# A hybrid attention trunk: a third early weight pair, gated linear attention as one stream, and later score scaling

## The chip, the cores and the metric

The kernel runs on one core of a Trainium2 chip. It is written as five instruction streams: PE (TensorE, matmuls and transposes into eight PSUM banks), DVE (VectorE), ACT (ScalarE), POOL (GpSimd) and SP (SyncE, which issues nearly all DMAs). The metric is the device time of one execution in microseconds; a profiled execution also gives a trace, whose span is a little shorter than the time.

## The reference

One layer over a sequence of 1024 tokens of width 1024, all in float32, cut to its core:

```python
h = rms_norm(x, pre_g)
qa, ka, va, ga, qb, kb, vb, gb, gk_low = split_columns(h @ w_in)     # 7184 columns

# 8 heads of differential softmax attention (two maps of width 64, values of 128)
w = softmax(causal(q1 @ k1.T)) - lam * softmax(causal(q2 @ k2.T))
oa = rms_norm(w @ va, subln_g) * (1 - lam_init) * silu(ga)

# 4 heads of gated linear attention (GLA; keys of 128, values of 256)
log_a = log_sigmoid(gk_low @ w_gk_up + b_gk) / 16
S_t = exp(log_a_t) * S_{t-1} + k_t^T v_t ;  o_t = q_t S_t
ob = rms_norm(o, gla_g) * silu(gb)

out = x + rms_norm(concat(oa, ob) @ w_out, post_g)
```

## The kernel before, in words

**Precision.** Every float32 operand of a large product is split into a rounded part `hi` (a cast by ACT) and the residue `lo` (a subtraction by DVE), and the product is three matmuls: hi by hi, lo by hi and hi by lo. A "residue" below is the DVE half of such a split, a "cast" the ACT half.

**Projections.** `h @ w_in` is computed by a scheme with seven products in place of eight for each 2x2 arrangement of blocks, numbered n = 1 to 7. The left operands are sums of blocks of h (`h11`, `h12`, `h22`, `s1` to `s4`), the right ones sums and differences of weight blocks. The *wide* steps (VB, VA: the values of GLA and of attention) multiply weight blocks of 512 columns, in two halves kk; their casts are L284, their residues L285, their differences L256. n = 6 needs a difference of its own tile, `w_t`. The *narrow* steps take a *pair*, two blocks of 128 columns of one kind: QA, KA, GA for attention's queries, keys and gates, QB, KB, GB for GLA's. A narrow step is 12 matmuls of 128x512 (L117). Its cast is L325, its residue L327; after it ACT copies the sum ("snap", L471) or DVE adds the parts, and `take` finishes them (L377 is the residue of the stored queries and keys, L381 their four DMA stores).

**Order of the work.** The list `order` fixes PE's order: four VB steps, then the early pairs' first two products, the rest of VB, VA, and then all other narrow steps. Pairs below `EARLY` = 2 load one 128-column half of their weights ahead of time (`load_early`, L220, tiles ks0 and ks1). `go(n)` does the next n steps and prepares the weights of about four steps to come; behind each narrow step it also advances one step of the stream in `fill`, and from pair `EARLY` on one step of loading, splitting and storing `w_out` (L644 to L652). The buffer of the raw weights, PSUM banks and the order in which each engine's code is written set the rest: each engine works through its own list and waits where a tile isn't ready.

**The gates of GLA.** `low_rank` (two matmul groups, the tiles gkl) and `decay(g)` (PE's `gk` from gkl, then ACT and DVE) run between the narrow steps, at 208 to 271 us.

**GLA.** `gla(g)` is a generator, one for each of four heads, chained into `fill`; each does two blocks (halves of the sequence): intra-chunk products `pa`, transposed keys `pk`, states `kv` (two groups), outputs `gpo` (two groups; ACT copies them to o at L904), and then the norm. The norm's mean over 256 channels is a matmul of `ones` with the squares: ACT squares both halves of o (L818, L821), DVE adds them, ACT casts the sum to `sq_hl` (L910), DVE takes the residue (L911), and after two more steps two matmuls of 128x512 give `gms`. Then ACT (L918, L920), DVE and ACT finish o, multiply by the gates and store hi and lo to `mixe` (L931, on SP). The tiles o and gates have one buffer each. The stream begins at the narrow step (7, 5); the first loads come at its first step.

**Scores and values.** After the last narrow steps the kernel merges by planned time three streams: the scores of all heads, the values, and the output product over the GLA half (`ypart`, from the tiles m_hi and m_lo that `mix` loads from `mixe`, L1000). For each block of 128 queries and each map m, PE makes the scores (`sc`), DVE adds the mask and finds the minimum in one instruction (L1109; the scores are negated), ACT takes the exponential with its sum (L1119). Then DVE takes the reciprocals of both sums (L1124), POOL scales the second map (L1125), and DVE scales the first and subtracts (L1128); the result is transposed on PE, cast and split (L1169) and multiplied by the values (`po`; the tiles v, loaded at L1060).

**The end.** From 942 us on the attention half of the output product (`yps`), the last norm and the stores.

Of the kernel before, what the change touches and what calls it, by code (L numbers as in the profile page):

```python
# [31 lines left out]
def hymba_kernel(  # L32
# [139 lines left out]
    pairs += [(n, h, c + h * P) for h in (2, 4) for n, c in (("KA", KA), ("QA", QA))]  # L172
# [18 lines left out]
    EARLY = 2  # L191
# [40 lines left out]
    def load_blocks(kind, *names):  # L232
        for name in names:
            r0, c0 = (512 * (int(i) - 1) for i in name)
            c0 += {"VA": VA, "VB": VB}[kind]
            for kk in range(2):
# [63 lines left out]
    def make_weights(i):  # L300
# [4 lines left out]
        if p in early and n < 3:  # L305
            src = early[p][n - 1]
        else:
# [384 lines left out]
    sums_of("s4")  # L692
    more_blocks("s1")
    go(1)
# [93 lines left out]
    low_rank()  # L788
    decay(0)
    go(4)  # L790
# [17 lines left out]
    go(order.index((4, 1)) - made[0])  # L808
# [6 lines left out]
    def mean_square(os, tile):  # L815

        sq = tile("sq")
        act.activation(sq, os[0], AF.Square)  # L818
        for o in os[1:]:
            sq2 = tile("sq")  # L820
            act.activation(sq2, o, AF.Square)  # L821
            dve.tensor_tensor(sq, sq, sq2, ALU.add)
        return sq

    loaded = {}

    def gla_loads(g, half):

        if g < GLA_HEADS and (g, half) not in loaded:
            cs = cols(half)  # L830
            kq = kp.tile([P, 2, 512], F32, tag="q0", name="kq")
            v = kp.tile([P, 4, 256], F32, tag="k0", name="gv")
            qd = kp.tile([P, 512], F32, tag="q1", name="gqd")
            sp.dma_start(kq[:, 0], gq_d[g][2, :, cs])
            sp.dma_start(kq[:, 1], gq_d[g][0, :, cs])
            c0 = g % 2 * 256
            sp.dma_start(v, gv_d[g // 2][:, half * 4 : half * 4 + 4, c0 : c0 + 256])
            sp.dma_start(qd, gq_d[g][1, :, cs])
            loaded[g, half] = kq, v, qd
        return loaded.get((g, half))  # L840

    def gla(g):

        u = None
        for half in range(2):
            cs = cols(half)
            kq, v, qd = gla_loads(g, half)
            gates = kp.tile([P, 2, 512], F32, tag="ks1", name="gg")
            o = kp.tile([P, 2, 512], F32, tag="ks0", name="go")
            an = kp.tile([P, 2, 4, P], F32, tag="k1", name="gan")  # L850
            a, kn = an[:, 0], an[:, 1]
            pa, ib = take_bank([P, 4, P], "pa")
# [8 lines left out]
            yield  # L861
            pk, ib = take_bank([P, 4, P], "pk")
            for i in range(4):
                tr(pk[:, i, :], kq[:, 0, i * P : i * P + P])
            free.append(ib)
            act.copy(kn, pk)
            for t in range(2):
                sp.dma_start(gates[:, t], gg_d[g][t, :, cs])
            yield
            us = [u]  # L870
            for m in range(2):
# [18 lines left out]
                yield  # L890
            for m in range(2):
# [15 lines left out]
            gla_loads(*((g, 1) if half == 0 else (g + 1, 0)))  # L907
            sq = mean_square([o[:, 0], o[:, 1]], t_c)
            hl = kp.tile([P, 2, 512], F32R, tag="k1", name="sq_hl")
            act.copy(hl[:, 0], sq)  # L910
            dve.tensor_tensor(hl[:, 1], sq, fp(hl[:, 0]), ALU.subtract)  # L911
            yield
            yield
# [656 lines left out]
```

## Time and profile before

| | |
|---|---|
| three runs, us | 1004.08, 1006.36, 1007.86 (median 1006.36) |
| profiled execution | 1009.11 us, its span 1007.4 us |
| mean granted PE clock | 0.989 |
| PE busy | 970.2 us, 4874 matmuls and transposes |
| DVE, ACT, POOL busy | 733.7, 586.3, 150.8 us |
| DMA | 219.86 MB, 218 GB/s |
| wide steps of the values | 14 to 190 us |
| GLA (pa to the last copy of o) | 333 to 581 us |
| scores | 637 to 941 us |
| end (yps) | 942 to 1000 us |

A row of a group of instructions gives line, engine, operation, the tile written and those read, the count, and then busy time with the mean of one and the idle time of the engine ahead of them with what ended it. "PE gms L117 <- ACT sq_hl L910: 3.9, 2, 2.6" says that PE idled 3.9 us in all ahead of gms, twice, at most 2.6 us, until ACT had written sq_hl. A row of the chain or of a timeline gives the start, the duration, and in brackets the wait ahead of it. DMA rows give the time of the issue and, where asked, the time from issue to landing. A clock of 0.50 means that PE was granted half of its full clock there.

### The profile page before, as it was taken

Reading aid. Unit: us, or ns where it says so; the run is one execution under the profiler, and the core shown is the slowest. Engines: PE = TensorE matmul, PEld = TensorE weight load, DVE = VectorE, ACT = ScalarE, POOL = GpSimd, SP = SyncE. Lnnn points to the kernel's source line nnn. Section 1 sums busy time; section 2 is a strip of 40 time slices with the busy share of each in tenths; the row PEclk is TensorE's granted clock in tenths of the full one; section 3 lists DMA queues with packets and bytes.
Section 4 is the critical chain, followed back from the end, with each engine's and each line's share of the span. In section 5 each row is a group of like instructions: output and inputs, shape, how many; then the busy total and the mean of one; then the engine's idle time right before and its main releaser. Section 6 shows DMA issues by size and latency. Waiting matters only on the chain.

```text
span 1007.4 us, 14826 instructions
## 1 busy us (share of the span) xinstructions
PE 970.2 (96%) x4874; PEld 812.4 (81%) x4874; DVE 733.7 (73%) x1442; ACT 586.3 (58%) x1144; POOL 150.8 (15%) x153
## 2 busy tenths in 40 slices
PE   6989999999999999999899999989999999999987
PEld 4868888778878788888788788778888888888765
DVE  6985476889898687777767884667777777887545
ACT  8631232455673587555566773457667667777663
POOL 5400000000000000001100100012222222343242
PEclk9999999999999999999999999999999999999999
DMA  9534333746657775898888789996575589974477
GB/s 335 181 93 150 122 110 104 234 135 193 235 180 257 234 240 193 273 297 268 252 262 251 230 253 324 310 350 187 164 230 199 178 286 369 275 200 91 128 219 136
DMA packets 155789, 219.86 MB, mean 218 GB/s; under 512 B 16208, under 2 KB 82768, under 8 KB 155616
## 3 DMA queue, kind: packets, MB, share of 16 engines
q1 hardware_dynamic: 151680, 211.57, 64.7%
q0 software_dynamic: 4032, 7.34, 4.8%
q8 instruction: 38, 0.62, 0.2%
q14 instruction: 39, 0.32, 0.1%
HBM read 133.41 MB, written 88.60 MB: 220 GB/s over the span
## 4 chain that ended last, share of the span: by engine, by line
PE 76%; DMA 9%; DVE 7%; ACT 3%; issue 2%; SPq 1%; POOL 1%; DVEq 0%; ACTq 0%; POOLq 0%
PE v L117 15%; PE x L117 13%; PE ypart L117 11%; PE y L117 8%; PE z L117 8%; PE sc L117 6%; PE po L117 4%; PE yps L117 4%; PE wtr L120 2%; PE gpo L117 2%; DMA v<-v_d 2%; PE kv L117 1%; DMA wo_raw<-in_w_out_dram 1%; DMA m_lo<-mixe 1%; PE gkl_ps L117 1%
## 5 line engine op out<-in xcount | busy, mean ns | idle before, releaser
L1119 ACT ACTIVATE p<-p,stt 128x896 f32<-128x896 f32 (+7 forms) x128 | 99.4, 777 | 47.2 <-DVE stt L1109 45.9
L327 DVE TENSOR_TENSOR w<-w_raw,w 128x512 fp32r<-128x512 f32 x136 | 94.4, 697 | 31.1 <-ACT w L325 30.9
L325 ACT CAST w<-w_raw 128x512 fp32r<-128x512 f32 x136 | 83.8, 620 | 51.1 <-PE y L117 31.9
L1109 DVE CUSTOM_DVE_ANT_0 p<-sc,maskt 128x512 f32<-128x512 f32 (+3 forms) x128 | 74.5, 585 | 31.4 <-PE sc L117 30.4
L1125 POOL TENSOR_SCALAR p<-p,stt,lam 128x1024 f32<-128x1024 f32 (+3 forms) x64 | 54.9, 863 | 241.5 <-DVE stt L1124 240.2
L117 PE MATMUL v<-w,s_hi 128*128 128x512 f32 x256 | 81.0, 396 | 3.7 <-ACT w L284 2.3
L117 PE MATMUL x<-s_hi,w 128*128 128x512 f32 x320 | 81.6, 398 | 0.7 <-ACT s L471 0.7
L117 PE MATMUL y<-h_hi,w 128*128 128x512 f32 x320 | 80.6, 394 | 0.0
L117 PE MATMUL z<-s_hi,w 128*128 128x512 f32 x320 | 80.5, 393 | 0.0
L117 PE MATMUL ypart<-wo_hi,m_hi 128*128 128x512 f32 x192 | 80.1, 417 | 0.0
L117 PE MATMUL ypart<-wo_hi,m_lo 128*128 128x512 f32 x192 | 76.4, 398 | 0.4 <-DMA m_lo<-mixe 0.4
L117 PE MATMUL ypart<-wo_lo,m_hi 128*128 128x512 f32 x192 | 76.2, 397 | 0.0
L117 PE MATMUL sc<-k,q 128*128 128x512 f32 (+1 forms) x192 | 71.2, 373 | 2.0 <-DVE stt L1109 2.0
L858 POOL TENSOR_SCALAR_AFFINE_SELECT gan<-gan 128x512 f32<-128x512 f32 x8 | 16.6, 2076 | 371.5 <-ACT gan L857 371.5
L117 PEld LDWEIGHTS x<-s_hi,w 128*128 128x128 f32 x320 | 59.8, 191 | 13.1 <-ACT s L471 1.1
L471 ACT COPY s<-x 128x512 f32<-128x512 f32 x60 | 35.0, 583 | 58.2 <-PE x L117 55.3
L117 PEld LDWEIGHTS z<-s_hi,w 128*128 128x128 f32 x320 | 59.1, 188 | 11.7
L117 PEld LDWEIGHTS y<-h_hi,w 128*128 128x128 f32 x320 | 59.0, 188 | 11.7
L117 PE MATMUL sc<-ks,q 128*128 128x512 f32 (+1 forms) x192 | 67.1, 351 | 0.0
L284 ACT CAST w<-w_block 128x1024 fp32r<-128x1024 f32 x24 | 25.1, 1052 | 69.1 <-PE v L117 39.8
L1128 DVE SCALAR_TENSOR_TENSOR p<-p,stt,p 128x1024 f32<-128x1024 f32 (+3 forms) x64 | 52.7, 826 | 15.8 <-POOL p L1125 15.3
L117 PEld LDWEIGHTS po<-wt_hi,v 128*128 128x128 f32 x320 | 54.1, 188 | 10.3 <-issue 2.2
(219 smaller groups left out, 2391.0 us busy)
## 6 DMA issues: line engine op xcount, KB each, us to landing
w_raw<-in_w_in_dram SPq DMA_DIRECT2D x40, 512.0 KB, 5.1
w_block<-in_w_in_dram SPq DMA_DIRECT2D x16, 512.0 KB, 4.4
k_d<-qk_st SPq DMA_DIRECT2D x64, 128.0 KB, 3.3
q_d<-qk_st SPq DMA_DIRECT2D x64, 128.0 KB, 3.4
wo_raw<-in_w_out_dram SPq DMA_DIRECT2D x32, 256.0 KB, 3.0
wo_d<-wo_hi SPq DMA_DIRECT2D x32, 256.0 KB, 2.8
wo_d<-wo_raw SPq DMA_DIRECT2D x32, 256.0 KB, 3.3
q<-q_d SPq DMA_DIRECT2D x32, 256.0 KB, 5.6
```

The lines of the kernel that those rows point to most:

```text
L117: tc.keep_in_program_order(pe.matmul(*a, **k))
L120: tc.keep_in_program_order(pe.transpose(dst, src, ident))
L284: act.copy(w[0], src)
L325: act.copy(w[0], src)
L327: split_last[:] = [dve.tensor_tensor(w[1], src, fp(w[0]), ALU.subtract)]
L471: act.copy(b[k], ps)
L858: pool.affine_select(a, a, [[0, 4], [1, P]], ALU.is_ge, 0.0, base=0, channel_multiplier=-1)
L1109: ins = dve.tensor_tensor_reduce(p[:, a:e], sc[:, : e - a], maskt[:, NZ + P - (e - a) :] if last else maskt[:, : e - a], 1.0, 3e38 if i == ...
L1119: act.activation(p[:, :n], p[:, :n], AF.Exp, bias=st[:, m : m + 1], scale=-1.0, accum_out=st[:, 2 + m : 3 + m],)
L1125: pool.tensor_scalar(p1[:, :n], p1[:, :n], st[:, 5:6], lam, ALU.mult, ALU.mult)
L1128: dve.scalar_tensor_tensor(p0[:, :n], p0[:, :n], st[:, 4:5], p1[:, :n], ALU.mult, ALU.subtract)
```

## The change

It has five parts.

1. *Early pairs.* `EARLY` is 3 and KA's second pair (heads 2 and 3) is the third early one, so its products 1 and 2 are the third couple of narrow steps between the wide steps of VB. Its early load uses the tile of pair 0 again and is issued once pair 0's second product is prepared. The wide blocks 12 and 22 are loaded kk by kk. `more_blocks` and the gates of GLA are shifted by some steps (`go`).
2. *GLA as one stream.* One generator `gla()` goes through the eight blocks. The first loads come two steps ahead of the first block, `pk` before `pa`, and the norm of a block (`gla_norm`) after the next block's `kv` groups, one step before its `gpo` groups. The tiles of o and gates are taken after that norm. The stream begins at step (8, 5).
3. *Squares.* The sum of the squares over 128 partitions is folded to 64; hi stands in the lower 64 partitions of one tile of 512 columns, lo in the upper 64, and one matmul replaces two. The tile is half of the next block's q tile.
4. *First values.* The values of the first head are loaded ahead of `mix(1)`.
5. *Scaling.* Reciprocal, POOL's scaling and DVE's scale and subtract of a block are issued when the next block's first minimum is (`scale_scores`).

The diff, cut to its core:

```diff
-    pairs = [("KA", 0, KA), ("QA", 0, QA), ("QB", 0, QB), ("KB", 0, KB), ("GB", 0, GB)]
+    pairs = [("KA", 0, KA), ("QA", 0, QA), ("KA", 2, KA + 256), ("QB", 0, QB), ("KB", 0, KB), ("GB", 0, GB)]
...
-    EARLY = 2
+    EARLY = 3
...
-        r = kp.tile([P, 2, HB, P], F32, tag=f"ks{p}", name="w_early")
+        r = kp.tile([P, 2, HB, P], F32, tag=f"ks{p % 2}", name="w_early")
...
     def load_blocks(kind, *names):
-        for name in names:
...
-            for kk in range(2):
+        for kk in range(2):
+            for name in names:
...
         if p in early and n < 3:
             src = early[p][n - 1]
+            if (p, n) == (0, 2):
+                load_early(2)
...
     sums_of("s4")
+    go(2)
     more_blocks("s1")
-    go(1)
+    go(2)
     more_blocks("s4")
...
     low_rank()
+    go(3)
     decay(0)
-    go(4)
+    go(5)
     decay(1)
...
+    def gla_norm(g, half, o, gates, hl):
+
+        ms, ib = take_bank([P, 512], "gms")
+        mm(ms, ones, hl, start=True, stop=True)
+        r = t_c("r")
+        act.activation(r, ms, AF.Ln, bias=eps_t, scale=1.0 / 256)
+        free.append(ib)
+        act.activation(r, r, AF.Exp, scale=-0.5)
...
+    def gla():
+
+        norm = None
+        gla_loads(0, 0)
+        yield
+        yield
+        for g, half in [(g, half) for g in range(GLA_HEADS) for half in range(2)]:
...
+            if norm:
+                gla_norm(*norm)
+                yield
+            gates = kp.tile([P, 2, 512], F32, tag="ks1", name="gg")
+            for t in range(2):
+                sp.dma_start(gates[:, t], gg_d[g][t, :, cs])
+            o = kp.tile([P, 2, 512], F32, tag="ks0", name="go")
...
-            hl = kp.tile([P, 2, 512], F32R, tag="k1", name="sq_hl")
-            act.copy(hl[:, 0], sq)
-            dve.tensor_tensor(hl[:, 1], sq, fp(hl[:, 0]), ALU.subtract)
+            hl = gla_loads(*((g, 1) if half == 0 else (g + 1, 0)))[2][:, 1]
+            sq, up2 = t_c("sq"), t_c("sq")
+            act.activation(sq, o[:, 0], AF.Square)
+            act.activation(up2, o[:, 1], AF.Square)
+            dve.tensor_tensor(sq, sq, up2, ALU.add)
+            act.copy(up2[:64], sq[64:])
+            dve.tensor_tensor(sq[:64], sq[:64], up2[:64], ALU.add)
+            act.copy(hl[:64], sq[:64])
+            dve.tensor_tensor(hl[64:], sq[:64], fp(hl[:64]), ALU.subtract)
+            norm = g, half, o, gates, hl
             yield
-            yield
-            ms, ib = take_bank([P, 512], "gms")
-            for i in range(2):
-                mm(ms, ones, hl[:, i], start=(i == 0), stop=(i == 1))
...
-    go(order.index((7, 5)) - made[0])
-    fill.append(chain(*(gla(g) for g in range(GLA_HEADS))))
+    go(order.index((8, 5)) - made[0])
+    fill.append(gla())
...
             if h == 0:
-                tc.keep_in_program_order(ins)
+                v_last[:] = [tc.keep_in_program_order(ins)]
...
-                if last and m:
-                    dve.reciprocal(st[:, 4:6], st[:, 2:4])
...
+                if last:
+                    c += scale_scores(ins)
+                    if m:
+                        unscaled.append((h, qb, n, st, p0, p1))
                 yield c
...
+    def scale_scores(after):
+
+        if not unscaled:
+            return 0.0
+        h, qb, n, st, p0, p1 = unscaled.pop()
+        with tc.issue_after(after.ins) if after else nullcontext():
+            dve.reciprocal(st[:, 4:6], st[:, 2:4])
+            pool.tensor_scalar(p1[:, :n], p1[:, :n], st[:, 5:6], lam, ALU.mult, ALU.mult)
+            dve.scalar_tensor_tensor(
+                p0[:, :n], p0[:, :n], st[:, 4:5], p1[:, :n], ALU.mult, ALU.subtract
+            )
+        w[h, qb] = p0
+        return 0.25 + n / 1024 * 1.4
...
             if e == E:
-                nxt = mix(1)
+                with tc.issue_after(v_last[0].ins):
+                    nxt = mix(1)
```

How it moves the instructions shows at three places. The first is ACT in GLA, around the norm of an early block (go is o, gg the gates, r the norm's factor). Before:

```order
L904 COPY go<-gpo 128x2x256
L818 ACTIVATE sq<-go 128x512
L821 ACTIVATE sq<-go 128x512
L471 COPY s<-x 128x512
L910 CAST sq_hl<-sq 128x512
L325 CAST w<-w_raw 128x512 x2
L471 COPY s<-x 128x512
L325 CAST w<-w_raw 128x512
L918 ACTIVATE r<-gms,eps_t 128x512
```

And now:

```order
L843 ACTIVATE r<-gms,eps_t 128x512
L845 ACTIVATE r<-r 128x512
L473 COPY s<-x 128x512
L327 CAST w<-w_raw 128x512
L852 CAST gg<-go 128x512 x2
L327 CAST w<-w_raw 128x512
L932 COPY go<-gpo 128x2x256 x2
L473 COPY s<-x 128x512
```

Before, the norm followed its own block's copies of o; now the norm of the block before stands directly ahead of the copies, which write the same tile o.

The second is SP at the start of the scores. Before:

```order
L381 DMA k_d<-qk_st 64x512 x4
L381 DMA q_d<-qk_st 64x512 x4
L1000 DMA m_hi<-mixe 128x1024
L1000 DMA m_lo<-mixe 128x1024
L1060 DMA v_5841<-v_d 128x1024
L1060 DMA v_5842<-v_d 128x1024
L950 DMA k_6030<-k_d 128x512 x2
```

And now:

```order
L383 DMA k_d<-qk_st 64x512 x4
L383 DMA q_d<-qk_st 64x512 x4
L1074 DMA v_5844<-v_d 128x1024
L1074 DMA v_5845<-v_d 128x1024
L1014 DMA m_hi<-mixe 128x1024
L1014 DMA m_lo<-mixe 128x1024
L964 DMA k_6024<-k_d 128x512 x2
```

The two loads of the first values and the two of `mix(1)` have changed places.

The third is DVE at the third block of the first head (ISA is the masked minimum, in two parts; wt_lo is the residue of transposed weights). Before:

```order
L1124 RECIPROCAL stt<-stt 128x2
L1169 TENSOR_TENSOR wt_lo<-wtr,wt_hi 128x512
L1109 ISA p_5964,stt<-sc,maskt 128x512
L1109 ISA stt 128x1
L1128 SCALAR_TENSOR_TENSOR p_5933<-p_5933,stt,p_5934 128x768
```

And now:

```order
L1124 ISA p_5963,stt<-sc,maskt,stt 128x128
L1124 ISA stt 128x1
L1152 RECIPROCAL stt<-stt 128x2
L1154 SCALAR_TENSOR_TENSOR p_5927<-p_5927,stt,p_5928 128x768
L1193 TENSOR_TENSOR wt_lo<-wtr,wt_hi 128x512
```

Before, this block's scaled product stood behind the next block's minimum and another product's residue; now it stands right behind its reciprocal, and both stand behind the minimum of the next block's first map.

More of the change, by code (lines that the diff above doesn't have):

```diff
@@ L805, in hymba_kernel @@
     dve.tensor_scalar(lam, lam, LAM_INIT, None, ALU.add)
-    go(order.index((4, 1)) - made[0])
+    go(order.index((5, 1)) - made[0])
     go(1)
@@ L812, in hymba_kernel @@
     decay(3)
[L815 to L823, printed above, removed]
     loaded = {}
     def gla_loads(g, half):
-        if g < GLA_HEADS and (g, half) not in loaded:
-            cs = cols(half)
[L831 to L849, printed above, removed]
+        if (g, half) not in loaded:
+            qh = kp.tile([P, 2, 512], F32R, tag="q1", name="gqd")
+            loaded[g, half] = [None, None, qh]
+            if g < GLA_HEADS:
+                cs = cols(half)
+                kq = kp.tile([P, 2, 512], F32, tag="q0", name="kq")
+                v = kp.tile([P, 4, 256], F32, tag="k0", name="gv")
+                sp.dma_start(kq[:, 0], gq_d[g][2, :, cs])
+                sp.dma_start(kq[:, 1], gq_d[g][0, :, cs])
+                c0 = g % 2 * 256
+                sp.dma_start(v, gv_d[g // 2][:, half * 4 : half * 4 + 4, c0 : c0 + 256])
+                sp.dma_start(fp(qh[:, 0]), gq_d[g][1, :, cs])
+                loaded[g, half][:2] = kq, v
@@ L860, in gla @@
             )
-            yield
[L862 to L868, printed above, removed]
             yield
```

69 lines of the change are left out of this document (35 added, 34 removed).

## The prediction

> **What bounds the kernel now.** I read the page first, then the waits of the matmul engine (PE), then the stages in which it idles. Three lines of the page:
>
> ```profile
> span 1007.4 us, 14826 instructions
> PE 970.2 (96%) x4874; PEld 812.4 (81%) x4874; DVE 733.7 (73%) x1442; ACT 586.3 (58%) x1144; POOL 150.8 (15%) x153
> PE 76%; DMA 9%; DVE 7%; ACT 3%; issue 2%; SPq 1%; POOL 1%; DVEq 0%; ACTq 0%; POOLq 0%
> ```
>
> PE is busy 96% of the span, so a change can win only where PE stands still, or by giving it fewer matmuls. The waits of PE over the whole run (us in total, times, longest):
>
> ```profile
> PE xT L120 <- DVE x L524: 9.2, 4, 7.7
> PE gms L117 <- ACT sq_hl L910: 3.9, 2, 2.6
> PE po L117 <- DMA v<-v_d: 2.8, 2, 2.0
> PE v L117 <- ACT w L284: 2.3, 1, 2.3
> PE sc L117 <- DVE stt L1109: 2.0, 3, 1.2
> ...
> PE v L117 <- DVE w L285: 1.3, 3, 0.8
> PE kv L117 <- DMA gv<-gv_d: 1.0, 1, 1.0
> ...
> PE gk L117 <- DVE gkl L753: 0.7, 1, 0.7
> ...
> PE gms L117 <- DVE sq_hl L911: 0.4, 2, 0.2
> ...
> PE pa L117 <- DMA kq<-gq_d: 0.3, 1, 0.3
> ```
>
> The first row is the start, which the change leaves alone. The other nine are each aimed at by one part of the change: together 3.9 + 2.8 + 2.3 + 2.0 + 1.3 + 1.0 + 0.7 + 0.4 + 0.3 = 14.7 us. That isn't all, as stretches of 3.41 us show (us, busy time of PE, PEld, DVE, ACT, POOL, granted PE clock, DMA share, GB/s):
>
> ```profile
> 57.33:60.74 3.41, 3.41 (x10) 2.63 (x9) 2.45 (x3) 0.93 (x1) 0.00 (x0) 0.50 0.58 133
> 490.82:494.23 3.41, 3.41 (x7) 2.44 (x8) 3.07 (x5) 2.78 (x5) 0.00 (x0) 0.50 0.86 259
> 555.67:559.08 3.41, 2.12 (x8) 1.53 (x9) 3.27 (x6) 3.39 (x7) 0.00 (x0) 1.00 0.59 189
> 647.84:651.25 3.41, 1.91 (x10) 1.21 (x9) 2.21 (x10) 1.19 (x3) 1.08 (x1) 1.00 0.79 184
> 651.25:654.66 3.41, 3.41 (x13) 2.83 (x12) 2.08 (x5) 2.21 (x5) 0.00 (x0) 0.50 0.89 251
> 661.49:664.90 3.41, 3.41 (x11) 2.62 (x10) 0.78 (x3) 0.91 (x2) 0.88 (x1) 0.50 1.03 311
> 668.00:940.00 272.00, 270.94 (x1581) 235.80 (x1580) 206.96 (x565) 192.20 (x425) 80.58 (x87) 1.00 0.72 221
> ```
>
> Four stretches run at clock 0.50, each right behind one of these waits; each gives PE half of 3.41 us of work and so costs another 1.7 us, 6.8 in all. A stretch in which PE was busy for 1.91 us was followed by one, a stretch with 2.12 us was not, so about 1.5 us of idle time in one stretch sets it off. The Trainium skill (TensorE: Matmul & The Clock Gate, HAM oscillation — how this bites in real kernels) states the rule as "no PE-idle gaps >~3.4µs". Here no gap of these stages is longer than 2.6 us and the clock fell nonetheless, so the trace speaks for the stricter reading; by the rule the clock would have nothing to give back. The last row tells that from 668 to 940 us PE idles for 1.1 us of 272: nothing is to be won there, only lost.
>
> **A third early pair.** Two more steps of 12 matmuls stand between the second early pair and the first difference weights w_t. PE and DVE there, from the chain and DVE's timeline:
>
> ```profile
> 41.63 2.74 PE x L117 x12
> ```
> ```profile
> 35.63 1.29 DVE L327 TENSOR_TENSOR w<-w_early,w 128x512 fp32r<-128x512 f32 x2
> 55.68 1.22 DVE L285 TENSOR_TENSOR w<-w_t,w 128x1024 fp32r<-128x1024 f32 x1 [0.51 <-ACT w L284]
> 57.96 0.68 DVE L377 SCALAR_TENSOR_TENSOR qk_st<-s,qk_st 128x512 fp32r<-128x512 f32 x1
> 68.78 1.22 DVE L285 TENSOR_TENSOR w<-w_block,w 128x1024 fp32r<-128x1024 f32 x1
> ```
>
> Two steps are 5.5 us of PE work that was done later in any case. DVE gets two residues of 0.65 us ahead of w_t, so w_t, finished at 56.9, comes at 58.2; PE, ready at 53.0, comes at 58.5. The waits there (2.3 and most of the 1.3) and the half clock behind them go, 5.3 us in reach. What is late next is the weights finished at 70.0 (the last row): DVE is 2.7 us later there (two residues, one sum, one 0.68 us residue of qk_st), PE only 58.5 + 10.9 - 69.0 = 0.4; one sum of 0.7 now follows instead of preceding them. I leave 1.0 us of wait: **-4.3**, between -5.3 and -2.6 (all of DVE's 2.7 us on the path). The early load shares the buffer of the first pair and is issued when DVE has read that, at about 37 us, ahead of the w_block loads of 45; its stores (four more SP issues) stand behind those loads. The wider order of those loads can only bring w_t earlier. A third x bank leaves one spare bank for the wide products instead of two; I price that at nothing, as the drains were done over 0.9 us before such a bank would be asked for, and a late drain costs its delay.
>
> **The low-rank gates.** Three steps (8.2 us) now stand ahead of the gk matmul: **-0.7**, at worst 0.
>
> **GLA.** The loads of the first block get two steps of cover, so the kq and gv waits go: **-1.3** (0 at worst). With hi and lo of the squares in two halves of one matmul, eight matmuls of 2.74 / 12 = 0.23 us fall away: **-1.8**. DVE and ACT get one small instruction more per block, off the path. The norm's matmul now stands behind the next block's four state products, about 20 us after its squares instead of two steps, so the gms waits (3.9 + 0.4) and the half clock of 490.82 go: -6.0. In return o and the gates, one buffer each, are handed from norm to next block within one step. The rows that price this: PE's wait and chain, then the tile `go` around that norm, then the landing of its stores (min, median, max) there and, last, over all blocks.
>
> ```profile
> 490.82 1.52 PE L117 MATMUL gms<-sq_hl,ones 128*128 128x512 f32 x2 [2.63 <-ACT sq_hl L910]
> ```
> ```profile
> 379.28 1.78 PE gpo L117 x16
> ```
> ```profile
> L931 SPq DMA_DIRECT2D mixe<-go x2: 394/461/528, 501.7 to 502.1; - x2
> ...
> DMA to landing us min/median/max: 2.7/2.8/2.9
> ```
> ```profile
> L904 ACT COPY go<-gpo x16: 566/577/588, 350.5 to 580.9; 128x512 f32<-128x512 f32 x16
> ...
> DMA to landing us min/median/max: 2.7/5.1/7.8
> ```
>
> The last store of that norm landed at 502.1 + 2.8, 14.1 us after its gms; with the slowest landing 19. In the new order ACT's copy of o waits for that, and behind it on ACT stand two squares, a snap, a cast and the copy of the next keys: about seven instructions of 0.6, 4 us. The keys are wanted six steps, two gpo groups, pk and pa after gms: 16.4 + 3.6 + 0.9 = 21 us. Usually 18 against 21 (no wait), at the slowest 23 against 21. Of seven hand-overs I charge +2.0 in all, between 0 and 7. GLA with the matmuls: **-7.1**, between -9.1 and -2.1.
>
> **First values ahead of mix.** SP issues (start, us) and the PE rows that want these loads; the landing row is m_lo's:
>
> ```profile
> 651.99 0.58 SPq L1000 DMA_DIRECT2D m_hi<-mixe  x1
> 652.61 0.44 SPq L1000 DMA_DIRECT2D m_lo<-mixe  x1
> 653.09 0.91 SPq L1060 DMA_DIRECT2D v<-v_d  x2
> ```
> ```profile
> DMA to landing us min/median/max: 5.0/5.0/5.0
> ```
> ```profile
> 659.33 0.35 PE L117 MATMUL po<-wt_hi,v 128*128 128x256 f32 x1 [1.99 <-DMA v<-v_d]
> 660.50 0.38 PE L117 MATMUL po<-wt_hi,v 128*128 128x256 f32 x1 [0.81 <-DMA v<-v_d]
> ...
> 665.52 0.40 PE L117 MATMUL ypart<-wo_hi,m_hi 128*128 128x512 f32 x1
> ```
>
> The values take the places of the mix loads and land by 657.6 instead of 660.5; PE wanted them at 657.3. So 2.8 us and the half clock of 661.49 go, 4.5 in reach. The mix loads then land at 660.5, and their first user, at 665.52, comes 4.5 us earlier, at 661.0: just in time. I charge +1.0: **-3.5**, between -4.5 and 0.
>
> **Scores scaled one block later.** DVE in this stage, by line, and one of its waits:
>
> ```profile
> L1128 DVE SCALAR_TENSOR_TENSOR p<-p,stt,p 128x1024 f32<-128x1024 f32 (+3 forms) x64 | 52.7, 826 | 15.8 <-POOL p L1125 15.3
> L1124 DVE RECIPROCAL stt<-stt 128x2 f32<-128x2 f32 x64 | 10.4, 162 | 19.5 <-ACT p L1119 19.1
> ```
> ```profile
> 645.52 1.28 DVE L1128 SCALAR_TENSOR_TENSOR p<-p,stt,p 128x1024 f32<-128x1024 f32 x1 [1.33 <-POOL p L1125]
> ```
>
> The reciprocal's wait for the exponential (19.5 us on DVE) mostly goes, but in the new order the reciprocal and the product that needs POOL's answer stand side by side in 39 of 64 blocks instead of 11, and each such pair waits about 1 us for POOL: some 30 us instead of 15.8. On DVE that cancels. On PE 2.0 us of sc waits and the half clock of 651.25 are in reach; but the first pair (645.52) waits as before, and the first transposes want a product that now stands behind one block more. **0**, between -3.7 and +2.0.
>
> **The sum.** -4.3 - 0.7 - 1.3 - 5.8 - 3.5 + 0 = -15.6, with -5.8 for gms (-6.0 - 1.8 + 2.0). The profiled execution took 1009.11 us (span 1007.4 and 1.7 around it) and would take 993.5. It is 2.75 us above the median of the three runs, 1006.36; the difference carried over to the median gives 990.8, forecast **991**.
>
> **Rivals.**
> 1. *Slower: ACT blocked at the copy of o.* For it: the order above, and stores that wait in SP's queue behind loads. Against: 18 against 21 us. It decides from a landing 17 us after gms on; at 20.5 PE would wait about 3.5 us in each of seven blocks and run a stretch at half clock after each: 7 x (3.5 + 1.7) = 36, less the 2.0 charged: 991 + 34 = 1025; slower than before from 2.5 us per block on. Chance 0.05.
> 2. *The stall moves from the values to the mix loads, and the scores cost 2.0.* For it: half a microsecond of room at 661.0, a DMA share of 1.03. Then 3.5 and 2.0 are lost: 996.5. Chance 0.17.
> 3. *The half clock isn't the waits' doing* (the reading of the rule above): it stays in the three stretches that I count as gone, 3 x 1.7: 996. Against it: all four stretches follow a wait. Chance 0.05.
> 4. *New waits eat it all*: the drains at one spare bank, and stores of the wo weights, which now start one pair later, among the loads before 635 us. The rows don't show such a wait; 1006. Chance 0.08.
>
> **How the numbers follow.** The forecast has 0.65. A measurement of this kernel can tell about 0.5% (5 us) from no change, so faster means under 1001.3. With rivals 2 and 3 that is 0.87, less a little for their upper ends: 0.86 faster, 0.09 same, 0.05 slower. With every term at its good end (-5.3 - 0.7 - 1.3 - 7.8 - 4.5 - 3.7 = -23.3) it is 983; the range runs from 984 to 1000, which takes in rivals 2 and 3 and leaves out 1 and 4.
>
> **What would show it.** Right: no gms wait, the v wait at w_t under 1.5 us, no po wait for v, clock 0.50 in at most two stretches between 50 and 700 us, 4866 matmuls. Wrong: waits at kv or pk for ACT, ypart waiting for m_hi or m_lo by over 2 us, or sc and wtr waits that sum to over 5 us from 640 to 940.

## The result, and the profile after

The changed kernel is slower: 1016.99 us in the median of 6 runs (1013.92 to 1020.77) against 1006.93 us of before (6 runs), a ratio of 1.0105 with a 95% interval of 1.0073 to 1.0137. The forecast was 991 us. The profiled execution took 1016.52 us, its span is 1014.8 us. Three lines of its page:

```profile
span 1014.8 us, 14875 instructions
PE 967.4 (95%) x4866; PEld 809.3 (80%) x4866; DVE 737.2 (73%) x1450; ACT 589.1 (58%) x1152; POOL 142.0 (14%) x153
...
PE 67%; DMA 17%; DVE 8%; ACT 4%; issue 3%; SPq 1%; POOL 0%; DVEq 0%; ACTq 0%; POOLq 0%
```

PE has its eight matmuls fewer and 2.8 us less work, but the span is 7.4 us longer: PE stands still 10 us more. In the chain of work that ended last (the third line) the share of DMA has gone from 9% to 17%. The waits of PE over the whole run (us in total, times, longest):

```profile
PE xT L120 <- DVE x L526: 8.5, 4, 7.1
PE ypart L117 <- issue: 5.5, 1, 5.5
PE gms L117 <- DVE gqd L943: 4.7, 2, 4.1
PE kv L117 <- ACT go L932: 3.3, 1, 3.3
PE kv L117 <- DMA gv<-gv_d: 2.7, 1, 2.7
PE yps L117 <- ACT yps L1447: 2.2, 2, 1.9
PE sc L117 <- DMA ks<-k_d: 2.1, 2, 1.5
PE wtr L120 <- DVE p L1154: 1.7, 1, 1.7
...
PE sc L117 <- DVE stt L1124: 1.4, 1, 1.4
...
PE v L117 <- DVE w L285: 0.5, 1, 0.5
```

Of the rows at which the change was aimed, v at the weights of ACT, gk, po for v and kq are gone, v at DVE is 0.5 instead of 1.3. In their place stand new rows, in two stretches of the program.

**GLA.** The new waits kv <- ACT go (3.3) and gms (4.7) belong to one ring: from the norm's matmul over its stores, the copy of o and its squares to the next norm's matmul. The third, kv <- gv (2.7), comes by another path (run 7). The waits of ACT between 340 and 640 us, after and then before, name the ring's closing point:

```profile
ACT go L932 <- DMA mixe<-go: 24.8, 6, 7.8
```
```profile
ACT go L904 <- DMA mixe<-go: 1.0, 1, 1.0
```

In six of the seven hand-overs ACT stood in front of the copy of o until the stores of the norm before had landed. The hand-over with the longest landing, first on ACT's timeline, then on PE's:

```profile
557.71 0.59 ACT L879 COPY gan<-pk 128x512 f32<-128x512 f32 x1
564.71 1.07 ACT L932 COPY go<-gpo 128x512 f32<-128x512 f32 x2 [6.41 <-DMA mixe<-go]
```
```profile
565.35 1.16 PE L117 MATMUL kv<-gv,gan 128*128 128x128 f32 x8 [3.30 <-ACT go L932]
573.04 0.47 PE L117 MATMUL gms<-gqd,ones 128*128 128x512 f32 x1 [0.59 <-DVE gqd L943]
597.59 0.63 PE L117 MATMUL gms<-gqd,ones 128*128 128x512 f32 x1 [4.13 <-DVE gqd L943]
```

The norm's matmul before this copy was at 540.8; the last store of o landed 23.8 us later. Over the seven blocks it was 13.5, 16.3, 17.1, 18.7, 18.9, 23.8 and 16.4 us. Then come the copies, two squares, the fold and the residue, and with them the next gms can run: from one gms to the end of the residue for the next the ring takes 22 to 32 us, and a block without waits has some 28.5. The first row of ACT shows that the block's keys had been copied ahead of the copy of o here, so it wasn't the keys that PE waited for at kv. That the copies had to free a PSUM bank for kv would explain the row, but isn't shown. The last row, 4.13 us, is the ring at the last block, which has only two plain steps ahead of its norm.

**Start of the scores.** The two parts of `mix(0)` are issued at 633.4 and 634.6 us and land 9.8 and 9.9 us later, behind ten loads of wo, each of 512 KB. PE waits 5.5 us for the first (the profile names "issue", but m_hi lands at 643.2 and the matmul starts at 643.27). Stretches of 3.41 us (us, busy time of PE, PEld, DVE, ACT, POOL, granted PE clock, DMA share, GB/s):

```profile
560.25:563.66 3.41, 1.79 (x8) 1.14 (x7) 0.00 (x0) 0.00 (x0) 0.00 (x0) 1.00 1.07 370
563.66:567.07 3.41, 1.72 (x12) 1.59 (x13) 0.70 (x2) 2.36 (x5) 0.00 (x0) 1.00 0.91 269
567.07:570.49 3.42, 3.42 (x19) 2.87 (x18) 3.42 (x5) 2.83 (x6) 0.89 (x1) 1.00 0.64 236
...
594.38:597.79 3.41, 0.20 (x1) 0.21 (x2) 3.35 (x7) 3.28 (x7) 0.00 (x0) 1.00 0.26 98
597.79:601.20 3.41, 3.41 (x9) 2.63 (x9) 3.41 (x6) 3.19 (x7) 0.00 (x0) 0.50 0.47 157
...
638.72:642.13 3.41, 0.00 (x0) 0.00 (x0) 0.69 (x1) 0.46 (x1) 0.00 (x0) 1.00 1.02 417
642.13:645.54 3.41, 1.81 (x4) 1.14 (x5) 0.00 (x0) 0.00 (x0) 0.00 (x0) 0.51 0.75 263
645.54:648.96 3.42, 3.42 (x10) 2.65 (x9) 0.70 (x2) 0.00 (x0) 0.00 (x0) 0.50 1.02 292
```

The half clock is gone from 57 and 490 us, where the waits went, and has come behind the new ones (597.79; two stretches from 642.13). While PE stood still from 638.72 to 642.13 the DMA engines were full.

### The profile page after: what moved, and what is told of

Read it like the earlier page. It is cut to its first block, busy times and chain, and to the rows that moved or that the text cites. A ratio compares the mean times of both kernels' runs of the same rounds, so it can differ in the third digit from the quotient of the medians.

```text
span 1014.8 us, 14875 instructions
## 1 busy us (share of the span) xinstructions
PE 967.4 (95%) x4866; PEld 809.3 (80%) x4866; DVE 737.2 (73%) x1450; ACT 589.1 (58%) x1152; POOL 142.0 (14%) x153
## 4 chain that ended last, share of the span: by engine, by line
PE 67%; DMA 17%; DVE 8%; ACT 4%; issue 3%; SPq 1%; POOL 0%; DVEq 0%; ACTq 0%; POOLq 0%
PE v L117 12%; PE ypart L117 11%; PE x L117 10%; PE z L117 7%; PE y L117 6%; PE sc L117 6%; PE po L117 5%; PE yps L117 4%; PE wtr L120 3%; DMA mixe<-go 2%; DMA v<-v_d 2%; DMA wo_d<-wo_raw 2%; DMA wo_raw<-in_w_out_dram 2%; DMA m_lo<-mixe 2%; DMA ks<-k_d 1%
## 5 line engine op out<-in xcount | busy, mean ns | idle before, releaser
L329 DVE TENSOR_TENSOR w<-w_raw,w 128x512 fp32r<-128x512 f32 x134 | 91.4, 686 | 27.2 <-ACT w L327 26.7
L327 ACT CAST w<-w_raw 128x512 fp32r<-128x512 f32 x134 | 82.6, 619 | 39.4 <-PE y L117 19.0
L256 DVE TENSOR_TENSOR w_raw<-w_raw 128x512 f32<-128x512 f32 x80 | 55.9, 699 | 11.2 <-DMA w_raw<-in_w_in_dram 10.2
L117 PE MATMUL v<-w,h_hi 128*128 128x512 f32 x192 | 60.3, 401 | 0.7 <-ACT h_hi L567 0.7
L887 POOL TENSOR_SCALAR_AFFINE_SELECT gan<-gan 128x512 f32<-128x512 f32 x8 | 7.1, 888 | 383.7 <-ACT gan L886 383.7
```

Source lines behind the costliest of these rows:

```text
L117: tc.keep_in_program_order(pe.matmul(*a, **k))
L256: dve.tensor_tensor(dst, a, b, ALU.subtract)
L327: act.copy(w[0], src)
L329: split_last[:] = [dve.tensor_tensor(w[1], src, fp(w[0]), ALU.subtract)]
L887: pool.affine_select(a, a, [[0, 4], [1, P]], ALU.is_ge, 0.0, base=0, channel_multiplier=-1)
```

## The experiments

All ratios are against the kernel before on the same chip, with 95% intervals; 0.1% is 1.0 us. "A" is the changed kernel. The parts taken one by one, each on the kernel before (the stream with its folded squares, which were not tried by themselves; the last row is two parts together):

| run | ratio | interval |
|---|---|---|
| early_pair_alone (with w_out earlier) | 1.0019 | 0.9989 to 1.0048 |
| stream_as_changed | 1.0033 | 1.0008 to 1.0059 |
| stream_norm_first | 0.9939 | 0.9907 to 0.9972 |
| values_alone | 0.9948 | 0.9919 to 0.9978 |
| scores_alone | 1.0048 | 1.0027 to 1.0068 |
| early_and_values | 1.0019 | 0.9997 to 1.0041 |

And from A on, one edit after the other:

| run | ratio | interval |
|---|---|---|
| A | 1.0105 | 1.0073 to 1.0137 |
| wout_from_early | 1.0095 | 1.0054 to 1.0136 |
| gla_as_before | 1.0080 | 1.0047 to 1.0112 |
| norm_before_states | 1.0016 | 0.9981 to 1.0050 |
| wout_and_norm | 0.9988 | 0.9953 to 1.0023 |
| mix_ahead_of_values | 0.9986 | 0.9966 to 1.0006 |
| mix0_ahead_of_wo | 0.9987 | 0.9964 to 1.0010 |
| scores_in_two_steps | 1.0070 | 1.0039 to 1.0101 |
| scores_as_before | 0.9926 | 0.9898 to 0.9953 |
| best_again (the same kernel) | 0.9953 | 0.9934 to 0.9973 |
| best_mix_first | 0.9963 | 0.9942 to 0.9983 |
| best_mix0 | 0.9956 | 0.9935 to 0.9978 |
| two_kept_alone | 0.9951 | 0.9931 to 0.9972 |

The theory ahead of the first runs: the hand-over of o (H) and the later stores of w_out (W) make the new waits. Rivals stand in each expectation.

**1. w_out earlier.** The prediction's fourth rival named the stores of w_out, which start one pair later.

```diff
-            if order[i][0] >= EARLY:
+            if order[i][0] >= EARLY or order[i][1] in (5, 6):
                 wo_step(order[i][1])
```

> The changed kernel, but the early pairs' products 5 and 6 also advance the steps that load, split and store w_out, so that the last store of w_out comes a few narrow steps earlier than in the kernel before instead of one pair later. Theory W (the late stores of w_out stand on SP ahead of the loads of wo, and these hold back m_hi): the matmul ypart waits under 1.5 us for m_hi instead of 5.5, the half clock there goes, 1017 - 8 = 1009 us. Rival N (SP is held by the ks loads, whose tiles are those of the last block's o and gates, so by the late last norm): ypart still waits 4 us or more, 1015 to 1017 us.

1017.45 us, no gain. PE waits at ypart for 2.5 + 0.8 us here, less than in A though more than W had it, but the time is that of A: W is refused as the cause. Rival N, with 4 us or more at ypart, isn't borne out either. What was gained at ypart doesn't reach the end, a first sign of what follows under 5.

**2. The norm ahead of the next states.** Two steps earlier, with the same number of steps in a block:

```diff
             yield
+            if norm:
+                gla_norm(*norm)
+                yield
             us = [u]
             for m in range(2):
...
-            if norm:
-                gla_norm(*norm)
-                yield
             gates = kp.tile([P, 2, 512], F32, tag="ks1", name="gg")
```

> The changed kernel, but the norm of a block stands ahead of the next block's two state groups (kv) instead of behind them, two steps earlier. Theory H (the hand-over of o: ACT's copy of o waits until the stores of the norm before have landed, 24.8 us in six copies, and that ripples on to kv, gms and the clock): ACT waits under 8 us at these copies, PE's waits for kv <- ACT go (3.3), gms (4.7) and the half clock behind (1.7) go, 1007 to 1009 us, and the last norm is about 8 us earlier. Rival S (the squares are then the late ones, with three steps less behind them): gms waits of 1 to 3 us in most blocks, 1015 to 1025 us.

1007.09 us: by the ratios 9 us less than A, for a norm two steps earlier. The waits of PE from 330 to 635 us in this kernel (the first is at the end of that time, at ypart):

```profile
PE ypart L117 <- DMA wo_d<-wo_hi: 4.8, 1, 4.8
...
PE gms L117 <- DVE gqd L943: 1.6, 3, 1.1
...
```

The kv waits are gone and gms is down to 1.6. But ACT still waits 21.7 us at the copies (seven, at most 4.8), not under 8 as expected: the copies follow the landing here too, only that PE doesn't meet them. The theory's place was right, its picture of how the wait goes was not: the copies still wait, but PE comes to what hangs on them later than they do.

**3. GLA of before, and both edits.** The first takes GLA's functions from the kernel before, the second has both edits above.

```diff
-    fill.append(gla())
+    fill.append(chain(*(gla(g) for g in range(GLA_HEADS))))
```

> The changed kernel with the GLA of the kernel before (one generator for each head, norm behind its own block, two matmuls for its squares); the other parts stay. Theory H: the stream costs 7 us more than the old one, and part of the wait for m_hi hangs on its late last norm: 1006 to 1010 us. If only the stores of w_out set that wait, 1010 us with ypart waiting 4 to 5 us; if the last norm sets it, 1002 us with ypart waiting under 1 us.

1013.37 us, above all its cases: A without its stream is still 8 us slower than before, and PE waits 3.6 us for m_hi. So the late last norm isn't the only cause of that wait.

> Both edits, w_out from the early pairs on and the norm ahead of the states. Theories W and H together: 1017 - 8 - 9 = 1000 us. If the transfers between 605 and 645 us are bound by the DMA engines themselves (share 1.0) and not by the order of the issues, ypart still waits 3 us or more and the time is 1004 us or more.

1004.14 us, and PE still waits 2.7 + 0.9 us at ypart. The second case holds: the transfers stay late.

**4. The scores.** The base is wout_and_norm (1004 us), with the scaling of before:

```diff
-                if last:
-                    c += scale_scores(ins)
-                    if m:
-                        unscaled.append((h, qb, n, st, p0, p1))
+                if last and m:
+                    dve.reciprocal(st[:, 4:6], st[:, 2:4])
...
```

> The kernel with w_out from the early pairs on and the norm ahead of the states (1004 us), and in it the scaling of the scores as in the kernel before. Theory P (the later scaling costs PE the waits sc <- DVE stt 1.4 and wtr <- DVE p 1.7 at the start of the scores, ks waits of 2.3 with a half clock near 860 us, and 1 us at the end): those rows go, 999 us. Rival: the waits only change their name (sc <- DVE stt three times, 2.0, as before), 1004 us.

999.21 us, the expected time, 0.6% under its base; but these are four runs, and twelve more of the same kernel (best_again, run 5) are 0.35% under it, with intervals that overlap. Of the rows that theory P names, ks fell from 2.3 to 0.8 us and yps <- yps from 2.1 to 0.8; wtr only changed its name (1.7, now 1.9 <- DVE stt). By itself on the kernel before:

> The kernel before with the later scaling of the scores alone. Theory P (DVE now waits for POOL in 40 of 64 blocks, 39 us in place of 14 plus 19 for the reciprocal, and PE meets the start and the end of the scores later for it): 1007 + 5 = 1012 us, with waits at sc, wtr and yps of over 5 us where there were 3.3. Rival (the later scaling costs only where PE is ahead of its transfers, which it isn't in the kernel before): 1006 to 1008 us.

1012.17 us: 0.48% slower, clear of noise (2.7 to 6.8 us). The waits of PE that have grown behind 700 us, with the later scaling (in an execution of 1008.19 us):

```profile
PE sc L117 <- DMA ks<-k_d: 1.7, 1, 1.7
PE yps L117 <- ACT yps L1431: 2.0, 1, 2.0
```

The first is at 864 us, the second at 941, with a clock of 0.83 from 940 to 950. In the kernel before PE waits nowhere from 850 to 900 us, and at most 0.7 us at yps <- yps. A and wout_and_norm, which have the later scaling too, show the same two places (1.5 and 1.9, 2.3 and 2.1). Counted by the matmuls in the trace, this kernel is 25 ahead of before at 850 us and 3 at 950; wout_and_norm is 3 ahead of scores_as_before at 850 us and 29 behind at 950. So it is there that the later scaling loses time. At the first transposes of scores_alone PE doesn't wait. How the later product delays the ks load isn't shown. The third run parts the reciprocal from the product by another minimum:

```diff
+                if last and not m:
+                    scale_second(ins)
-                if last:
+                if last and m:
                     c += scale_scores(ins)
-                    if m:
-                        unscaled.append((h, qb, n, st, p0, p1))
+                    unscaled.append((h, qb, n, st, p0, p1))
```

> The 1004 us kernel (w_out from the early pairs on, norm ahead of the states, later scaling), with the later scaling in two steps: reciprocal and POOL's product behind the next block's first minimum, DVE's product behind its second. Theory P1 (the later scaling costs because reciprocal and product stand side by side and DVE waits 39 us for POOL): DVE's waits for POOL fall under 10 us with the reciprocal's still under 5, and the time is at or under that of the kernel with the old scaling, 996 to 999 us. Rival P2 (it costs because the product, and with it the transposes, comes one block later): 1004 us or more, with DVE's waits gone all the same.

1016.19 us, worse by 0.8%. DVE's waits from 640 to 935 us, of its base wout_and_norm and of this kernel:

```profile
DVE p L1154 <- POOL p L1153: 39.4, 40, 1.4
DVE p L1124 <- PE sc L117: 23.0, 39, 2.4
```
```profile
DVE p L1124 <- PE sc L117: 56.1, 78, 3.1
...
DVE p L1162 <- POOL p L1154: 6.9, 17, 0.9
```

and PE's largest wait from 600 us on there:

```profile
PE po L117 <- DVE wt_lo L1202: 6.7, 8, 1.6
```

DVE's 39.4 us at POOL shrink to 6.9, as the theory P1 wanted, and the kernel is slower. P1 as it was put falls: taking these waits away gave no time back. The run doesn't price them by themselves, as the product is later still in this kernel, by one map's minimum. The cost has grown with that, which speaks for P2. How the later product gets to PE (a values stream that trails the scores, with fewer matmuls to cover it; the row of po) is argued from one profile, not shown.

**5. Where the early pair's time goes.** The early pair by itself, with its `go` counts, and w_out as in 1:

```diff
-    EARLY = 2
+    EARLY = 3
...
-            if order[i][0] >= EARLY:
+            if order[i][0] >= EARLY or order[i][1] in (5, 6):
```

> The third early pair alone, with w_out from the early pairs on; GLA, values and scores as before. PE has 5 us less of waits by 220 us. Theory G (the transfers from 600 to 645 us give the end of the narrow steps its time, so that what PE gains ahead of them is waited off at ypart): ypart waits 3 us or more for m_hi, 1004 to 1006 us. Rival: the gain comes through, 1001 us or less.

1010.9 us. The matmuls of ypart and po, before and then with the pair (the shortest, median and longest in ns, the first and last start in us), and PE's wait at po with the pair:

```profile
L117 PE MATMUL ypart<-wo_hi,m_hi x192: 387/397/628, 635.4 to 937.1; 128*128 128x512 f32 x192
...
L117 PE MATMUL po<-wt_hi,v x320: 220/280/384, 659.3 to 959.3; 128*128 128x256 f32 x128, 128*128 128x128 f32 x32
```
```profile
L117 PE MATMUL ypart<-wo_hi,m_hi x192: 387/397/629, 631.2 to 939.1; 128*128 128x512 f32 x192
...
L117 PE MATMUL po<-wt_hi,v x320: 220/280/582, 659.0 to 961.7; 128*128 128x256 f32 x128, 128*128 128x128 f32 x32
```
```profile
PE po L117 <- DMA v<-v_d: 5.1, 2, 4.5
```

PE comes to the scores 4.2 us earlier and starts the values 0.3 us earlier: it waits 5.1 us for v, where it waited 2.8. The expected place was ypart, it was po; that the lead is given back at transfers is as theory G has it. But the time is above G's 1004 to 1006 us: from the first po to the last this kernel loses another 2.7 us, and that isn't explained. The next two kernels differ in the pair and the w_out edit: the stream with its norm ahead of the states, the folded squares, the values first and the old scaling, without the two and with them.

> The kernel before with GLA as one stream (norm ahead of the states), the folded squares and the first values ahead of mix; no third early pair, scores as before. It is the 999 us kernel without the early pair and without the change to w_out. Theory G (the transfers from 600 to 700 us set when the scores run, and what the early pair gains ahead of them is waited off): ypart doesn't wait for m_hi, 999 to 1001 us. Rival (the early pair's 5 us come through): 1004 us.

> The kernel that took 999 us (early pair, w_out from the early pairs on, norm ahead of the states, folded squares, values first, scores as before), in more rounds. 0.74% under the kernel before, with an interval of 0.3% either way; without the early pair it was 0.49%. Theory G (the early pair's gain is waited off): 0.4 to 0.6%, 1003 us; rival (it comes through where the rest is mended): 0.7 to 1.0%, 999 us.

1002.52 us and 1002.54 us, 0.9951 and 0.9953: the pair is worth nothing here, within some 0.3%, as G has it (whose 999 to 1001 us for the kernel without it were too low). The 999 us of scores_as_before, the same kernel, came from four runs; the two intervals overlap. PE's waits from 600 to 720 us, with the pair and then without it:

```profile
PE ypart L117 <- DVE qk_st L379: 2.3, 1, 2.3
PE wtr L120 <- DVE stt L1139: 1.9, 1, 1.9
PE ypart L117 <- DMA m_lo<-mixe: 1.3, 1, 1.3
PE sc L117 <- DMA ks<-k_d: 1.1, 2, 0.7
```
```profile
...
PE sc L117 <- DMA ks<-k_d: 0.3, 1, 0.3
```

With the pair PE is there early and waits up to 4.7 us for transfers, without it 0.3 us. (The first row ends at 631.81; m_hi landed at 631.8, the residue that the row names ended at 631.6, so both were late.)

**6. The order of the loads.** The values ahead of mix(1) alone, and on the early pair; then undone on wout_and_norm and on the best kernel:

```diff
-                with tc.issue_after(v_last[0].ins):
-                    nxt = mix(1)
+                nxt = mix(1)
```

> The kernel before with the first values ahead of mix(1), and nothing else. The prediction's term: v lands 2.8 us earlier, a half clock goes, 1007 - 3.5 = 1003 us. Theory G (transfers set this stretch; what v gains, m_hi, k or ks lose): 1006 to 1008 us.

1003.4 us: a gain of the size of the prediction's term (5.2 us, interval 2.2 to 8.2). Its mechanism isn't in the trace, though (of an execution of 1006.27 us, the longest of twelve). PE's wait for v there:

```profile
PE po L117 <- DMA v<-v_d: 2.0, 2, 1.2
```

It was 2.8 before, and behind it PE still runs at a clock of 0.69 from 660 to 665 us (0.66 before). What has gone is the half clock at 651, ahead of the values. So the size may be luck. Beside other parts the gain isn't there:

> The third early pair (w_out from the early pairs on) and the first values ahead of mix; GLA and scores as before. Without the values' part PE waited 5.1 us for v and ran 1.7 us at half clock behind it. Theory V: these go, 1011 - 5 = 1006 us. Theory G: the wait moves to m_hi, k or ks, 1009 us or more.

> The same kernel (1004 us), with mix(1) ahead of the first values, as before. Theory V (the order of these four loads is worth what the prediction said): PE waits 2 to 3 us for v at its first po, with a half clock behind, 1004 + 3.5 = 1007.5 us. Rival: the transfers of this stretch are so late in either order that the wait only moves between v and m_hi: 1004 us.

> The same kernel with mix(1) ahead of the first values. By itself the values' part gave 0.52%; beside the early pair alone nothing. Theory V (it is worth what PE stood at v): 5 us slower than the other of this call. Theory G (beside a stream that reaches this stretch earlier, m_hi and v are both late, and their order decides nothing): the same within 0.2%.

By the ratios 1.0019 against 1.0019, 0.9986 against 0.9988, and 0.9963 against 0.9953: no difference in all three. And `mix(0)` ahead of four of the twelve loads of wo:

```diff
-    for e in range(E, E + 6):
+    for e in range(E, E + 4):
         weights(e)
     go(2)
     mix0 = mix(0)
+    weights(E + 4)
+    weights(E + 5)
```

> The same kernel (1004 us), with mix(0) issued ahead of the last two of the first six pairs of wo loads. Theory Q (m_hi is late because it stands behind 12 loads of 512 KB that land 1.2 to 1.7 us apart): m_lo lands 5 to 6 us earlier, the waits of ypart for it (2.7 and 0.9) and two half clocks (3.4) go, 998 us. Rival (the DMA engines are full there, whatever the order): the wait moves to wo_hi of the fifth or sixth pair and to the k and q stores behind it, 1003 to 1005 us.

> The 999 us kernel (early pair, w_out from the early pairs on, norm ahead of the states, folded squares, values first, scores as before), with mix(0) ahead of the last two of six pairs of wo loads. Theory G: ypart starts 4 us earlier and the 4 us are waited off at v and ks before 710 us: 998 to 1000 us. Rival: the lead is kept, 995 us.

0.9987 against 0.9988 of the base, 0.9956 against 0.9953. In the first PE starts ypart 5.1 us earlier than its base (624.0 against 629.1), and the next waits take it (600 to 720 us):

```profile
PE sc L117 <- DMA ks<-k_d: 2.4, 2, 1.4
PE po L117 <- DMA v<-v_d: 2.0, 2, 1.2
```

**7. The stream by itself,** with the norm where the change has it, and two steps earlier.

> The kernel before with GLA as the change has it (norm behind the next states), and nothing else. Theory H (the loop from gms over the stores' landing, the copy of o and its squares to the next gms takes 22 to 31 us where a block has 28 to 30): kv, gms and their half clocks cost 8 to 10 us that the same stream with the norm ahead of the states doesn't pay, 1010 to 1012 us. Rival (the waits came from the other parts' transfers): 1003 us, like the other.

> The kernel before with GLA as one stream, norm ahead of the next states, and folded squares; nothing else. Theory H: the loop of o closes within a block's time, 8 matmuls less and no wait for kq or gv: 1007 - 4 = 1003 us. Rival (G, the stretch from 600 to 710 us takes it back): 1006 us.

1012.14 and 1002.9 us: the place of the norm decides 0.94%, 9.4 us. PE's waits from 330 to 635 us, as changed and then with the norm first:

```profile
PE kv L117 <- DMA gv<-gv_d: 7.9, 1, 7.9
PE gms L117 <- DVE gqd L939: 4.4, 2, 3.9
```
```profile
PE gms L117 <- DVE gqd L939: 3.5, 1, 3.5
...
```

So the ring at gms makes 0.9 us of the difference here, and the load of gv 7.9. Little of that is the ring's doing. SP as changed (the longest wait, the first and last store of the norm, the load), and the load with the norm first:

```profile
SPq L648 <- ACT wo_hi L644: 5.3, 1, 5.3
474.82 0.38 SPq L852 DMA_DIRECT2D mixe<-gg  x1
479.70 0.54 SPq L852 DMA_DIRECT2D mixe<-go  x1
488.33 0.54 SPq L829 DMA_DIRECT2D gv<-gv_d  x1
```
```profile
480.87 0.38 SPq L829 DMA_DIRECT2D gv<-gv_d  x1
```

SP stood 5.3 us at a store of w_out for ACT's cast, which itself had waited 4.0 us for the raw weights. Behind it stand the norm's four stores, among others, and then this load; with the norm first these four were issued by 468.8 us, ahead of the crowd. What the trace shows of the ring on SP is a store that waited 0.8 us for ACT behind the copy of o. A shows the same order at its wait of 2.7 us (5.0 us at the cast, the stores from 489.0, the load at 498.05). Whether the stand at the cast or the stores in between decides wasn't tried.

## Why the prediction was wrong

All three signs of being wrong that it names showed in A: a wait at kv for ACT (3.3), ypart waiting for m_hi (5.5), and waits at sc and wtr of 5.2 us from 640 to 940.

**The early pair** (forecast -4.3 and -0.7 for gk). Mechanism and size were right where they were worked out: the waits at w_t and at gk and the half clock at 57 are gone. The step that failed is the silent one behind it, that a microsecond won at 60 us is a microsecond at the end. Of the gain 4.2 us were left at 631 us, and 0.3 at 659 (run 5). The stretch ahead of that, in the kernel before:

```profile
595.00:650.00 55.00, 52.82 (x232) 42.73 (x230) 33.63 (x62) 25.42 (x45) 1.53 (x2) 1.00 0.94 315
```

The DMA engines have a share of 0.94 there. That what PE wants at its end comes when they have done it is argued from this, not shown.

**GLA** (forecast -7.1). Its removed waits were right: with the norm first the stream gives 6.1 us (interval 2.8 to 9.4). The term that failed is the +2.0, between 0 and 7, charged for seven hand-overs of o. With the norm behind the states, as the change has it, the stream costs 9.4 us more than with the norm ahead of them (run 7), in A 8.9 us (run 2). The working compared the landing (18 us) with the 21 us until PE wants the next keys, and so priced one reader only. Two others showed. The same copy also stands at the head of o's squares and so of the next gms; that ring, 22 to 32 us in a block of 28 to 30, was not followed round. And the norm's stores now stand on SP close ahead of the next gv load. How the 9 us divide between these two isn't settled: in A the ring's rows are the larger (3.3 + 4.7 against 2.7), in the stream by itself the load's (7.9).

The first rival had ACT's stand at the copy of o, which the trace shows, but neither its path nor its size. Behind the four landings above its 17 us (17.1, 18.7, 18.9 and 23.8) PE waited 0.5, 0, 0.6 and 3.3 us; only the first of these is for the keys.

**The values** (forecast -3.5). Alone the time fits, -5.2, but the mechanism isn't in the trace (run 6): v is still waited for, 2.0 us, and the half clock behind it is still there. As a summand the term failed. In A PE waits 5.5 us for m_hi ahead of that place, and by its first po, at 667.4 us, the v that it needs has landed. The second rival had the stall move to the mix loads; there is one, but at mix(0), which the change doesn't touch.

**The scores** (forecast 0, between -3.7 and +2.0). The term was mis-sized: +4.8 (2.7 to 6.8). The working counted DVE's waits (some 30 us expected, 39.6 measured) and let them cancel; in run 4 they go and no time comes back. "the first transposes want a product that now stands behind one block more" was in the text, and got no price. The runs put the cost elsewhere: at a ks load near 864 us and at the end's first yps, near 941, with half clock behind the second (run 4), the first of them in a stage for which the prediction had said that there was only something to lose.

**The sum.** The parts alone (the pair with w_out earlier) give +1.9, +3.3, -5.2 and +4.8 us, together +4.8, and A has 10.5; with the values' term at nothing, as beside the other parts, +10.0. That this sum fits is no proof of it; its four intervals are 0.2 to 0.3% wide to either side. The third rival is refused as far as the runs go: in A the half clock left the places whose waits left. The fourth gave 1006 and named the stores of w_out, which aren't the cause (run 1).

**The best version** is about 0.5% faster than before (best_again, 0.9953): the change with the norm two steps earlier, w_out from the early pairs on and the old scaling. The stream with the norm first gets there by itself, and so do the values alone; the two together (two_kept_alone, 0.9951) gave no more than either. What holds them at 1002 to 1003 us isn't settled: a PE that comes early to the stretch from 625 to 710 us waits for transfers there, but whether the rate of the DMA engines, the order on SP or the moment at which buffers come free sets their time wasn't told apart.

## What to carry to other kernels

When a buffer is handed from one stage to the next, follow the ring through both stages back to where it began, and compare it with the time of one round, not only with the first reader. Follow what the later stores push back in their queue, too. A gain in front of a stretch that transfers fill may be waited off there; price terms that aim at one such stretch together, not as a sum. An engine's waits that cancel say nothing about the engine that waits for its results.

## What the runs showed of the hardware that wasn't expected

The prediction read from before that a stretch of 3.41 us with PE busy for 1.91 us is followed by one at half clock, and one with 2.12 us is not. The rows above contradict the threshold: two stretches in a row with 1.79 and 1.72 us (560.25 and 563.66) were followed by a full clock. One with 0.20 us (594.38) was followed by 0.50. The Trainium skill (TensorE: Matmul & The Clock Gate, HAM oscillation — how this bites in real kernels) sets the bound at gaps of more than about 3.4 us. The wait of 3.30 us at 565.35 with a full clock behind it agrees with that, the wait of 2.63 us at 490.82 in the kernel before with half clock behind it does not. Nor does the length of a wait decide by itself: behind one of 2.67 us (kv at 503.66, after) the clock stayed full. Neither reading holds for all rows, and what else decides was not tried.
